# Expert stage: gate and value columns paired on a partition, one PSUM bank per expert, one-hots by comparison, one weight buffer fewer

## The chip, the cores and the metric

The kernel runs on one core of a Trainium2 chip. The metric is the device time of one execution in microseconds (us), median over runs. Before the change it is 1808.41 us (three runs, 1807.29 to 1809.11). In the profile PE is TensorE (matmuls and transposes), PEld its weight loads, DVE is VectorE, ACT is ScalarE, POOL is GpSimd, and SP is the engine whose queue issues the weight DMAs.

## The reference

The program computes two transformer blocks on 256 tokens of width 1024, with a context of 256 tokens, all in float32. The first block mixes retention and a long convolution and ends in a mixture of 32 experts, of which each token uses two. The second has two layers of its own. The change concerns the experts:

```
expert_id = g_star * EXPERTS_PER_GROUP + e_top
...
def expert_block(args):
    xblk, e = args
    return (jax.nn.silu(xblk @ w1[e]) * (xblk @ w3[e])) @ w2[e]
...
y = yb[dest] * sw[:, None].astype(u.dtype)
return jax.ops.segment_sum(y, stok, num_segments=n_tok)
```

`w1` and `w3` are 1024 by 512, `w2` is 512 by 1024, so one expert has 6 MB of weights and all 32 have 201 MB, each read once. The result is `x + gt2 * y`, then normed.

## The kernel before

**Order of the work.** `program` (L1745) runs the first block's mix, then `route_all` (L1021: positions and weights of every token for every expert) and `moe` (L1035: the experts), then the second block. While the experts run, `side()` puts one step of the generator `context_side` behind each expert: the context's layer of the second block. It is matmul work with split operands (`hh`, `hl`, `wh`, `wl`) that uses two PSUM banks of its own, "pf". The kernel is written in Tile, whose scheduler sets the order of each engine's instructions when the program is built; the hardware then runs each engine's list in that order.

**One expert** has up to 32 slots (tokens). `gather` (L945) makes, for a group of 4 or 8 experts (`GROUPS` 4, 4, 8, 8, 8), the one-hots `oh` of slots by comparing positions with a row of numbers, and with matmuls the slots' modulated rows `xg` [128 columns, 8, 32 n]. `expert` (L984) then does a first product of `xg` (stationary, 32 columns) with `w1` and `w3` (moving, 256 columns): 32 matmuls, four column blocks on four groups of 32 partitions. Since gate (`w1`) and value (`w3`) end on different partitions there, ACT copies the 128x256 result out (`eh`), PE transposes both halves into a second bank, ACT takes tanh (`eth`), DVE multiplies twice (`ex`), and the second product, 16 matmuls with `w2`, goes into a third bank. `put` (L1040) weights the result by slot weight and gate row (`ey`), splits it into `yh` and `yl`, and adds it to the four accumulators `acc` by matmuls with the scatter matrix `sc`.

`scatter_mat` (L969) makes `sc` for every expert: POOL copies the expert's one-hots four times over (`oh` 128x256), PE transposes them (two transposes), two matmuls with `wt` give the slots' weights `ws`, ACT copies both out.

**Banks.** `ps()` (L187) hands out PSUM tiles; in this stage it alternates two banks, "pm". An expert uses one for the first product, one for the transposes, one for the second product and one for `scatter_mat`, in turn.

**Weights.** `half` (L234) takes a buffer of 1 MB (128x2048), from a pool of 6 (`p16`) or one of `XB` = 4 more (`p16x`, made by `more_chunks`), and SP issues its load. An expert has six such halves; `w1`'s first, `w3`'s first, `w1`'s second, `w3`'s second, `w2`'s two. Each half of `w1` and `w3` holds four K tiles of 512 columns, and a buffer comes free after its last matmul. Halves of the context's layer take their turn in the same pools:

```
def half(self, src):
    self.nchunk += 1
    x = self.p16x and self.nchunk * self.nx % (6 + self.nx) < self.nx
    pool = self.p16x if x else self.p16
    t = pool.tile([P, 2048], F32, tag="T16", name=self.nm("w"))
    self.load(t, src)
    return t
```

SP's queue is in order: a load that waits for its buffer holds up all loads behind it. `phase` (L136) makes the other tile pools; `n2` is the number of 128x512 tiles of the stage (1 before).

## Time and profile before

| what | value |
|---|---|
| runs (us) | 1807.29, 1808.41, 1809.11 |
| profiled execution | 1809.11 us, its span 1809.1 us |
| PE / PEld busy | 1675.7 us (93%) / 1262.9 us (70%) |
| DVE / ACT / POOL busy | 982.5 us (54%) / 723.0 us (40%) / 97.1 us (5%) |
| granted clock of TensorE, mean | 0.975 |
| HBM | 487.43 MB read, 5.80 MB written, 273 GB/s |
| chain that ended last | PE 64%, DVE 4%, DMA 3%, issue 2%, ACT 2% |
| expert stage, first product of the first expert to end of the last | 466.6 to 1089.0 us |

The profiled execution is the slowest of the three runs, 0.7 us above the median; nothing lies outside its span. A line names the line of the kernel, the engine, the operation, output and inputs by their names in the program, and shapes. L200 is the helper that issues every matmul, L203 that of transposes, so tiles tell them apart: `pm<-w,xg` is a first product, `pm<-w,ex` a second, `pm<-ident,eh` the transposes of an expert's hidden columns, `pm<-ident,oh` and `pm<-wt,oh` the work of `scatter_mat`, `acc<-yh,sc` and `acc<-yl,sc` the sums, and `pf<-...` the context's layer. A float32 matmul stands as two or four records. "issue" as a releaser means that nothing the profile shows was waited for.

### The profile page before, as it was taken

To read this page: it belongs to the slowest core of one execution; us is meant where nothing else is said; L and a number is where in the kernel's file an instruction comes from. 1 tells how busy PE (TensorE), PEld (TensorE's weight loads), DVE (VectorE), ACT (ScalarE), POOL (GpSimd) and SP (SyncE) were. 2 spreads that over 40 slices of the span, in tenths; PEclk is the share of its full clock that TensorE was granted. 3 is DMA by queue.
4 is the path that set the end of the run, shared out by engine and by line. 5 is a ranking of instruction groups with operands and counts; after the bars stand their busy time and mean duration, and the time that the engine had idled before them with its cause. 6 is when DMAs were issued, how large, how long until landed. Compare 5 with 4: busy or idle time off the path is not lost.

```text
span 1809.1 us, 29140 instructions
## 1 busy us (share of the span) xinstructions
PE 1675.7 (93%) x11876; PEld 1262.9 (70%) x11876; DVE 982.5 (54%) x1747; ACT 723.0 (40%) x1246; POOL 97.1 (5%) x127
## 2 busy tenths in 40 slices
PE   5999999999888989999899989998999989979997
PEld 1678766668565556776676658775899768659996
DVE  5625556466224345454454457586655567755555
ACT  2413434343323333332232236463444445635443
POOL 0000000000000000000000002011000021110001
PEclk9899999998999999999999999999999999989998
DMA  9654678985799999899979997617555676235550
GB/s 372 265 210 163 229 268 314 345 314 211 298 420 420 405 396 369 335 422 420 399 304 422 406 378 226 213 66 285 210 192 190 232 229 204 98 111 190 191 189 35
DMA packets 79035, 495.18 MB, mean 274 GB/s; under 512 B 9024, under 2 KB 15840, under 8 KB 22832
## 3 DMA queue, kind: packets, MB, share of 16 engines
q1 hardware_dynamic: 73920, 475.94, 68.7%
q0 software_dynamic: 4000, 13.13, 2.8%
q10 hardware_dynamic: 976, 4.19, 0.6%
q8 instruction: 95, 1.56, 0.3%
q14 instruction: 44, 0.36, 0.1%
HBM read 487.43 MB, written 5.80 MB: 273 GB/s over the span
## 4 chain that ended last, share of the span: by engine, by line
PE 64%; DVE 4%; DMA 3%; issue 2%; ACT 2%; SPq 0%; ACTq 0%; DVEq 0%
PE pf L200 23%; PE pm L200 19%; PE acc L200 11%; PE pa L200 5%; PE pj L200 2%; PE pm L203 2%; DMA w<-in_w_in 1%; PE pf L203 1%; PE pada L200 1%; DMA w<-in_e 1%; DVE xn L213 0%; DVE x L1596 0%; DVE wl L273 0%; ACT eh L206 0%; DVE rq L218 0%
## 5 line engine op out<-in xcount | busy, mean ns | idle before, releaser
L206 ACT ACTIVATE wh<-w 128x1024 fp32r<-128x1024 f32 x350 | 367.2, 1057 | 399.8 <-PE pa L200 152.3
L273 DVE TENSOR_TENSOR wl<-w,wh 128x1024 fp32r<-128x1024 f32 x246 | 301.7, 1229 | 302.9 <-PE pa L200 100.3
L200 PE MATMUL pf<-hh,wh 128*128 128x256 f32 x592 | 168.4, 286 | 3.7 <-ACT wh L206 2.6
L200 PE MATMUL pf<-hl,wh 128*128 128x256 f32 x592 | 166.5, 283 | 0.0
L200 PE MATMUL pf<-hh,wl 128*128 128x256 f32 x592 | 165.1, 285 | 0.8 <-DVE wl L273 0.8
L209 DVE TENSOR_TENSOR wl<-w,wh 128x1024 fp32r<-128x1024 f32 x96 | 117.2, 1224 | 83.5 <-ACT a L206 29.5
L200 PE MATMUL pm<-w,xg 128*32 128x256 f32 x2048 | 133.0, 382 | 1.9 <-DMA w<-in_e 1.3
L200 PEld LDWEIGHTS pf<-hh,wh 128*128 128x128 f32 x592 | 113.2, 191 | 10.0 <-issue 4.1
L200 PEld LDWEIGHTS pf<-hh,wl 128*128 128x128 f32 x592 | 111.4, 191 | 3.7 <-DVE wl L273 1.2
L200 PEld LDWEIGHTS pf<-hl,wh 128*128 128x128 f32 x592 | 113.1, 191 | 1.0 <-issue 0.4
L200 PE MATMUL acc<-wl,hh 128*128 128x512 f32 x256 | 101.8, 398 | 0.0
L200 PE MATMUL acc<-wh,hl 128*128 128x512 f32 x256 | 101.3, 396 | 0.0
L200 PEld LDWEIGHTS pm<-w,xg 128*32 128x32 f32 x2048 | 64.8, 109 | 51.9 <-issue 11.9
L200 PE MATMUL pada<-w,csil 128*32 128x512 f32 x576 | 92.2, 621 | 5.0 <-DMA w<-in_ada_w 5.0
L200 PE MATMUL acc<-wh,hh 128*128 128x512 f32 x256 | 90.7, 396 | 0.0
L200 PE MATMUL pm<-w,ex 128*32 128x256 f32 x1024 | 65.2, 393 | 25.8 <-issue 24.1
L200 PE MATMUL pm<-hh,wh 128*128 128x256 f32 x256 | 72.4, 283 | 0.0
L200 PE MATMUL pm<-hl,wh 128*128 128x256 f32 x256 | 72.2, 282 | 0.0
L200 PE MATMUL pm<-hh,wl 128*128 128x256 f32 x256 | 72.0, 281 | 0.0
L200 PEld LDWEIGHTS pm<-w,ex 128*32 128x32 f32 x1024 | 34.9, 112 | 47.5 <-issue 31.4
L200 PE MATMUL pf<-wl,hh 128*128 128x512 f32 x160 | 65.3, 408 | 1.0 <-DVE wl L209 1.0
L200 PE MATMUL pf<-wh,hl 128*128 128x512 f32 x160 | 63.2, 395 | 0.0
(500 smaller groups left out, 3487.9 us busy)
## 6 DMA issues: line engine op xcount, KB each, us to landing
w<-in_e SPq DMA_DIRECT2D x192, 1024.0 KB, 10.6
w<-in_ff SPq DMA_DIRECT2D x96, 1024.0 KB, 5.0
w<-in_ada_w SPq DMA_DIRECT2D x72, 1024.0 KB, 6.9
w<-in_w_in SPq DMA_DIRECT2D x54, 1024.0 KB, 8.3
w<-in_w_out SPq DMA_DIRECT2D x16, 1024.0 KB, 7.4
w<-in_ret_w_o SPq DMA_DIRECT2D x4, 1024.0 KB, 4.9
w<-in_w_su SPq DMA_DIRECT2D x3, 1024.0 KB, 4.9
adab<-in_ada_b SPq DMA_DIRECT2D x9, 256.0 KB, 12.7
```

The source lines that it names most:

```text
L200: self.nc.tensor.matmul(out, lhsT, rhs, start=start, stop=stop, skip_group_check=True)
L203: self.nc.tensor.transpose(out, in_, self.ident)
L206: self.nc.scalar.activation(out, in_, f, **k)
L209: self.nc.vector.tensor_tensor(out, a, b, op=op)
L273: (self.nc.gpsimd if self.slow > 0 else self.nc.vector).tensor_tensor(lo[:, :w], src, hi[:, :w], op=ALU.subtract)
```

## The change

- **Weights.** `e1` and `e3` become one array `e13` [32, 128, 8192]. A K tile has 1024 columns, and blocks of 256 columns hold 128 gate and 128 value columns, so that gate and value of the same hidden column are on the same partition after the first product. A 1 MB half now holds two K tiles (8 matmuls), one half used after the other.
- **Expert.** ACT takes tanh of the gate columns from the first product (`eg`), DVE makes `eg` and `eh`, PE transposes once (128x128), into columns 256 to 384 of the same bank; DVE multiplies by `wr` (`ex`), the slots' weights on rows; the second product goes into columns 0 to 256 of the same bank. `ey` is a product with the gate row alone.
- **Scatter matrices.** `scatter_mats` makes them for two experts at once: two matmuls spread a row of `posT` (positions, transposed once in `route`) over all partitions, by a broadcast column of `pick`, and one DVE comparison with `slot` (the partition's number modulo 32) gives `sc` [128, 2, 256]. Copy, transposes and weight matmuls of `scatter_mat` go.
- **Slot weights.** `gather` multiplies the one-hots by `wt` (two DVE operations) and sums them over partitions with two matmuls with a column of 0.5 (the silu's factor), which ACT copies to `wr`.
- **Buffers.** `XB` goes from 4 to 3: nine weight buffers in the stage instead of ten. `n2` goes from 1 to 3. `overflow` (experts with over 32 tokens) reads `e13`.

The rest of the diff takes out comments and docstrings.

```
-XA, XB = 2, 4
+XA, XB = 2, 3
...
-        t = self.pr.tile([P, 512], F32, tag="AR", name="router")[:, :484]
+        t = self.pr.tile([P, 512], F32, tag="AR", name="router")[:, :485]
...
+        self.slot = t[:, 484:485]
...
+        p = self.ps()[:32, :256]
+        for t in range(2):
+            self.tr(p[:, t * P:(t + 1) * P], self.pos[:, t, :])
+        self.posT = self.keep([32, 256], F32R, "posT")
+        self.act(self.posT, p)
+        self.pick = self.keep([32, 32], F32R, "pick")
+        self.act(self.pick, self.ident[:32, :32])
...
-        return oh, xg
-
-    def scatter_mat(self, oh, e, i):
-        o4 = self.tx([P, 2, 4, 32], F32, "oh4")
-        self.nc.gpsimd.tensor_copy(o4, oh[:, :, i:i + 1, :].to_broadcast([P, 2, 4, 32]))
-        p = self.ps()
-        v = [o4[:, t].rearrange("p j c -> p (j c)") for t in range(2)]
         for t in range(2):
-            self.tr(p[:, t * P:(t + 1) * P], v[t])
+            self.tt(oh[:, t], oh[:, t], self.wt[:, t, es].unsqueeze(2).to_broadcast([P, n, 32]), ALU.mult)
+        p = self.ps()[:, :w]
+        half = self.sm([P, 1])
+        self.nc.vector.memset(half, 0.5)
         for t in range(2):
-            self.mm(p[:, 256:257], v[t], self.wt[:, t, e:e + 1], False, t == 1)
-        sc, ws = self.tx([P, 256], F32R, "sc"), self.sm([P, 1])
-        self.act(sc, p[:, :256])
-        self.act(ws, p[:, 256:257])
-        return sc, ws
-
-    def expert(self, xg, e, i, put):
+            self.mm(p, half.to_broadcast([P, P]), oh[:, t].rearrange("p e c -> p (e c)"), t == 0, t == 1)
+        wr = self.keep([P, 256], F32, "wr")
+        self.act(wr[:, :w], p)
+        return wr, xg
+    def scatter_mats(self, e):
+        p = self.ps().rearrange("p (i t) -> p i t", i=2)
+        for i in range(2):
+            self.mm(p[:, i], self.pick[:, e + i:e + i + 1].to_broadcast([32, P]), self.posT, i == 0, True)
+        sc = self.t2([P, 2, 256], F32R, "sc")
+        self.ts(sc, p, self.slot, None, ALU.is_equal)
+        return sc
+    def expert(self, xg, wr, e, i, put):
         a = self.a
-        w1, w3 = (Chunk([]) for _ in range(2))
-        for h in range(2):
-            for n, w in (("e1", w1), ("e3", w3)):
-                w.halves.append(self.half(a[n][e][:, 2048 * h:2048 * h + 2048]))
+        w13 = self.chunk(a["e13"][e], (P, 8192))
         w2 = self.chunk(a["e2"][e])
         p = self.ps()
         for k in range(8):
             for j in range(4):
-                w = (w1, w3)[j // 2]
-                o = k * 512 + (j % 2) * 256
-                self.mm(p[32 * j:32 * j + 32, :256], xg[:, k, 32 * i:32 * i + 32], w[:, o:o + 256], k == 0, k == 7)
-        h = self.tx([P, 256], F32, "eh")
-        self.act(h, p[:, :256])
-        p = self.ps()
-        for q in range(2):
-            self.tr(p[:, q * P:(q + 1) * P], h[:, q * P:(q + 1) * P])
-        pv = p[:, :256].rearrange("p (q w j c) -> p q w j c", q=2, w=2, j=2)
-        th = self.tx([P, 2, 2, 32], F32, "eth")
-        x1 = self.tx([P, 2, 2, 32], F32, "ex1")
-        self.act(th, pv[:, :, 0], AF.Tanh, scale=0.5)
-        self.stt(x1, th, 1.0, pv[:, :, 0], ALU.add, ALU.mult)
-        self.stt(x1, x1, 0.5, pv[:, :, 1], ALU.mult, ALU.mult)
-        p = self.ps()
+                o = k * 1024 + j * 256
+                self.mm(p[32 * j:32 * j + 32, :256], xg[:, k, 32 * i:32 * i + 32], w13[:, o:o + 256], k == 0, k == 7)
+        g, h = self.tx([P, P], F32, "eg"), self.tx([P, P], F32, "eh")
+        self.act(g, p[:, :P], AF.Tanh, scale=0.5)
+        self.stt(g, g, 1.0, p[:, :P], ALU.add, ALU.mult)
+        self.tt(h, g, p[:, P:256], ALU.mult)
+        q = p[:, 256:256 + P]
+        self.tr(q, h)
+        x1 = self.tx([P, 4, 32], F32, "ex")
+        self.tt(x1, q.rearrange("p (j c) -> p j c", j=4),
+                wr[:, 32 * i:32 * i + 32].unsqueeze(1).to_broadcast([P, 4, 32]), ALU.mult)
         for f in range(4):
             for j in range(4):
-                self.mm(p[32 * j:32 * j + 32, :256], x1[:, f % 2, f // 2, :],
+                self.mm(p[32 * j:32 * j + 32, :256], x1[:, f, :],
                         w2[:, f * 1024 + j * 256:f * 1024 + (j + 1) * 256], f == 0, f == 3)
         put(e, p)
...
-            self.stt(y, p[:, :256], ws, self.g4, ALU.mult, ALU.mult)
+            self.tt(y, p[:, :256], self.g4, ALU.mult)
...
-                        self.mm(acc[j][:, t], sc[r, t * P:(t + 1) * P], v[r], e == 0 and t == 0 and n == 0, e == 31)
+                        self.mm(acc[j][:, t], sc[r, e % 2, t * P:(t + 1) * P], v[r], e == 0 and t == 0 and n == 0, e == 31)
 
         e = 0
         for n in GROUPS:
-            oh, xg = self.gather(xn, A, B, e, n)
+            wr, xg = self.gather(xn, A, B, e, n)
             for i in range(n):
-                sc, ws = self.scatter_mat(oh, e, i)
-                self.expert(xg, e, i, put)
+                if i % 2 == 0:
+                    sc = self.scatter_mats(e)
+                self.expert(xg, wr, e, i, put)
...
-                        for n in ("e1", "e3"):
+                        for n in range(2):
                             w = tile_(1024, "w").rearrange("p (k c) -> p k c", k=8)
-                            self.load(w, a[n][ds].rearrange("o p (k h c) -> p (o k) h c", k=8, h=4)[:, :, f])
...
+                            self.load(w, a["e13"][ds].rearrange("o p (k m c) -> p (o k) m c", k=8, m=8)[:, :, 2 * f + n])
...
-            self.phase(es, 1, 0, 1, 5)
+            self.phase(es, 1, 0, 3, 5)
...
-                                    np.tile(rb, (P, 1))], 1)
-    d["e1"] = np.concatenate([_pack(w) for w in i["expert_w1"][0]])
-    d["e3"] = np.concatenate([_pack(w) for w in i["expert_w3"][0]])
+                                    np.tile(rb, (P, 1)), (np.arange(P, dtype=np.float32) % 32)[:, None]], 1)
+    both = np.stack([i["expert_w1"][0].reshape(32, 8, P, 4, P), i["expert_w3"][0].reshape(32, 8, P, 4, P)], 4)
+    d["e13"] = both.transpose(0, 2, 1, 3, 4, 5).reshape(32, P, 8192)
```

The build's order shows how the scheduler places this. PE, around the end of the first product of expert 27, before (`w_...` are halves, `ident_81` the identity for transposes):

```order
L200 MATMUL pm_9333<-w_9325,xg_8622 32x256 x2
L200 MATMUL pm_9333<-w_9327,xg_8622 32x256 x2
L203 MATMUL pm_9368<-ident_81,eh_9366 128x128 x2
L200 MATMUL pm_9376<-w_9329,ex_1759_9372 32x256 x8
L200 MATMUL pm_9376<-w_9331,ex_1759_9372 32x256 x8
...
L200 MATMUL pf_9420<-wh_9421,hl_9181 128x512
L203 MATMUL pm_9501<-ident_81,oh_1782_9499 128x128 x2
L200 MATMUL pm_9501<-wt,oh_1782_9499 128x1 x2
L200 MATMUL acc_3896<-yl_9396,sc_9317 128x256
```

Halves of `w1` and `w3` alternate, and three banks are in use. The same place in the changed program:

```order
L200 MATMUL pm_9066<-w_9056,xg_8389 32x256 x8
L200 MATMUL pm_9066<-w_9058,xg_8389 32x256 x8
L200 MATMUL pm_9066<-w_9060,xg_8389 32x256 x8
L200 MATMUL pm_9229<-posT,pick 128x256 x2
L203 MATMUL pm_9066<-ident_81,eh_9100 128x128
L200 MATMUL pm_9066<-w_9062,ex_9105 32x256 x8
L200 MATMUL pm_9066<-w_9064,ex_9105 32x256 x8
L200 MATMUL pf_9149<-wh_9151,hh_8924 128x512
```

The halves are used one after the other, one bank (`pm_9066`) serves the whole expert, and the two matmuls of the next pair's scatter matrices (`pm_9229`) stand between the first product and the transpose.

DVE in the same expert, before:

```order
L209 TENSOR_TENSOR hl_9181<-a_1744_9305,hh_9180 128x512
L218 SCALAR_TENSOR_TENSOR ex_1759_9372<-eth_9371,pm_9368 128x128
L218 SCALAR_TENSOR_TENSOR ex_1759_9372<-ex_1759_9372,pm_9368 128x128
L218 SCALAR_TENSOR_TENSOR ey_9393<-pm_9376,sm_9318,gate_520_2882 128x256
L209 TENSOR_TENSOR wl_9422<-w_9415,wh_9421 128x1024
L209 TENSOR_TENSOR yl_9396<-ey_9393,yh_9395 128x256
```

Nothing stands ahead of `ex` but the context's `hl`. And changed:

```order
L209 TENSOR_TENSOR hl_8925<-a_1621_9049,hh_8924 128x512
L213 TENSOR_SCALAR sc_9232<-pm_9229,router 128x512
L218 SCALAR_TENSOR_TENSOR eg_9099<-eg_9099,pm_9066 128x128
L209 TENSOR_TENSOR eh_9100<-eg_9099,pm_9066 128x128
L209 TENSOR_TENSOR ex_9105<-pm_9066,wr 128x128
L209 TENSOR_TENSOR ey_9123<-pm_9066,gate_520_2882 128x256
L209 TENSOR_TENSOR wl_9152<-w_9145,wh_9151 128x1024
L209 TENSOR_TENSOR yl_9126<-ey_9123,yh_9125 128x256
```

The comparison `sc` of the next pair stands ahead of this expert's `eg`. The same holds in experts 19, 21, 25 and 29; in the other odd experts it stands apart from this chain.

## Rows read from the trace of the kernel before

**Rows 1.** Page: busy time by engine; a DMA issue with KB and us to landing

```profile
PE 1675.7 (93%) x11876; PEld 1262.9 (70%) x11876; DVE 982.5 (54%) x1747; ACT 723.0 (40%) x1246; POOL 97.1 (5%) x127
...
w<-in_e SPq DMA_DIRECT2D x192, 1024.0 KB, 10.6
```

**Rows 2.** Busy time in stretches: PE, PEld, DVE, ACT, POOL, clock, DMA share, GB/s

```profile
500.00:525.00 25.00, 20.62 (x246) 14.83 (x246) 3.56 (x11) 5.28 (x15) 0.40 (x1) 1.00 1.01 420
...
750.00:775.00 25.00, 24.99 (x207) 20.23 (x210) 13.39 (x18) 6.58 (x11) 0.00 (x0) 1.00 0.76 307
...
950.00:975.00 25.00, 23.15 (x269) 16.22 (x268) 9.69 (x15) 8.41 (x16) 0.81 (x2) 1.00 1.01 422
```

**Rows 3.** Chain of waits, 466 to 1092: start us, us, what

```profile
504.78 19.76 DMA w<-in_w_in
...
660.71 15.95 DMA w<-in_e
```

**Rows 4.** Waits of PE, 466 to 1092: us in total, times, longest

```profile
PE pm L200 <- issue: 24.1, 19, 3.4
...
PE pm L203 <- ACT eh L206: 8.9, 19, 0.6
...
PE acc L200 <- ACT yh L206: 8.4, 14, 1.2
```

**Rows 5.** Timeline of PE in expert 27: start us, us, instruction, idle before

```profile
999.97 0.28 PE L200 MATMUL pf<-hl,wh 128*128 128x256 f32 x1
1000.09 0.28 PE L200 MATMUL pf<-hh,wl 128*128 128x256 f32 x1
...
1000.41 3.66 PE L200 MATMUL pm<-w,xg 128*32 128x256 f32 x64
1004.60 0.44 PE L203 MATMUL pm<-ident,eh 128*128 128x128 f32 x2 [0.53 <-ACT eh L206]
1006.10 1.93 PE L200 MATMUL pm<-w,ex 128*32 128x256 f32 x32 [1.06 <-issue]
...
1012.27 0.38 PE L203 MATMUL pm<-ident,oh 128*128 128x128 f32 x2
...
1012.92 0.39 PE L200 MATMUL acc<-yl,sc 32*128 32x256 f32 x4
```

**Rows 6.** Timeline of ACT in expert 27

```profile
1004.17 0.38 ACT L206 ACTIVATE eh<-pm 128x256 f32<-128x256 f32 x1 [1.77 <-PE pm L200]
1005.08 0.28 ACT L206 ACTIVATE eth<-pm 128x128 f32<-128x128 f32 x1 [0.53 <-PE pm L203]
```

**Rows 7.** Timeline of DVE in expert 27

```profile
1005.39 0.29 DVE L218 SCALAR_TENSOR_TENSOR ex<-eth,pm 128x128 f32<-128x128 f32 x1 [2.20 <-ACT eth L206]
1005.71 0.29 DVE L218 SCALAR_TENSOR_TENSOR ex<-ex,pm 128x128 f32<-128x128 f32 x1
1008.17 0.48 DVE L218 SCALAR_TENSOR_TENSOR ey<-pm,sm,gate 128x256 f32<-128x256 f32 x1 [2.17 <-PE pm L200]
```

**Rows 8.** Instructions by line and form, 466 to 1092: busy us, mean ns, idle before

```profile
L209 DVE TENSOR_TENSOR a<-pf,rowbc 128x512 f32<-128x512 f32 x36 | 24.8, 689 | 47.0 <-PE pf L200 47.0
...
L200 PE MATMUL pm<-oh,xn 128*128 128x256 f32 x96 | 23.2, 384 | 0.0
...
L215 DVE TENSOR_SCALAR xg<-pm,A,adac 128x256 f32<-128x256 f32 x12 | 6.5, 541 | 9.7 <-ACT xg L206 9.7
...
L215 DVE TENSOR_SCALAR xg<-pm,A,adac 128x128 f32<-128x128 f32 x4 | 1.6, 410 | 6.9 <-ACT xg L206 6.9
```

**Rows 9.** Timeline of SP's queue at two places; loads of the stage: first, last start

```profile
468.54 35.31 SPq L221 DMA_DIRECT2D w<-in_e  x20
...
949.87 1.55 SPq L221 DMA_DIRECT2D w<-in_e  x2
...
L221 SPq DMA_DIRECT2D w<-in_e x192: 327/328/1251, 388.4 to 1064.4; - x192
```

**Rows 10.** Timeline of PE where that load's first use stands

```profile
969.60 1.93 PE L200 MATMUL pm<-w,xg 128*32 128x256 f32 x32
```

More of the change, by code (lines that the diff above doesn't have):

```diff
@@ L832, in route_setup @@
     def route_setup(self, st):
-        t = self.pr.tile([P, 512], F32, tag="AR", name="router")[:, :484]
+        t = self.pr.tile([P, 512], F32, tag="AR", name="router")[:, :485]
         self.lsm(t, self.a["k_router"])
         self.iota, self.before = t[:, P:160], t[:, :P]
-        rw, rb = t[:, 160:448].rearrange("p (k n) -> p k n", k=8), t[:, 448:]
+        rw, rb = t[:, 160:448].rearrange("p (k n) -> p k n", k=8), t[:, 448:484]
+        self.slot = t[:, 484:485]
         self.A2, self.B2 = self.one([P, 8], F32, "A2", True), st[1][:, 0, 3, :]
@@ L1126, in overflow @@
                                 self.mm(ps, w[:, k], hT[:, k, :], k == 0, k == 7)
-                            if n == "e1":
+                            if n == 0:
                                 self.act(y[:, :P], ps, AF.Tanh, scale=0.5)
```

## The prediction

> **What bounds the kernel now.** I read the page first. [Rows 1] show TensorE (PE) busy for 93% of the span, so the questions are where PE stops and where the work that the change removes stands on PE's own path. The table of stretches comes next, because the change also takes a weight buffer away. [Rows 2] show three kinds of stretch in the expert stage: 500 to 525 us with the DMA at a share of 1.01 and 420 GB/s while PE is busy 20.6 of 25 us (weights are the limit), 750 to 775 with the DMA at 0.76 and PE at 25.0 (PE is the limit), and 950 to 975 with the DMA full again while PE has 23.2. The chain of waits says where weights end last: only two pieces of DMA stand in the chain of the whole stage, at 504.78 and 660.71 [rows 3]. So up to about 676 us (experts 0 to 12) the DMA sets the time, and from there to 1089 (experts 13 to 31) PE does, with the DMA catching up in its gaps.
>
> The waits of PE in the stage [rows 4] then say what its gaps are: 24.1 us in 19 gaps before an expert's second product, 8.9 us in 19 gaps before the transposes of its hidden columns, 8.4 us before the sums into `acc`. All three are the short chain inside an expert, which the change rewrites. Expert 27 shows it row by row [rows 5 to 7]. The first product ends at 1000.41 + 3.66 = 1004.07; ACT copies (0.38), PE transposes twice (0.44), ACT takes the tanh (0.28), DVE multiplies twice (0.29 each), and the second product starts at 1006.10: a chain of 2.03 us with nothing else on PE. Counted in PE's timeline, 14 of the experts 13 to 31 have this chain bare; in experts 13 to 17 rows of the context's layer stand in it and cover it.
>
> **The change part by part.**
> *Chain of an expert.* The copy of 256 columns and one transpose go; tanh now starts on the first product. In durations of [rows 5 to 7], with their hand-overs (0.11 PE to ACT, 0.03 on to DVE and between its operations, 0.05 to PE, 0.04 from PE, 0.10 from DVE to PE): 0.11 + 0.28 + 0.03 + 0.29 + 0.03 + 0.29 + 0.05 + 0.28 (one transpose; half of the pair is 0.22, so at most this) + 0.04 + 0.29 + 0.10 = 1.79. That is 0.24 less than 2.03.
>
> *Scatter matrices.* Two transposes and the weight column of one expert took PE from 1012.27 to 1012.92, 0.65 us [rows 5]. In their place each pair of experts has two single-pass matmuls of 256 columns; single-pass ones start 0.12 apart (999.97 to 1000.09, [rows 5]), so 0.24 a pair. The copy on POOL and the copies on ACT had slack and are worth nothing.
>
> *The new one-hot on DVE.* `sc` is one comparison of 128x512 from PSUM. It is not in the trace. Below: 0.69 (an operation of that size from PSUM); above: 0.80, since the tensor_scalar from PSUM went from 410 to 541 ns over 128 columns [rows 8], and 256 more columns add 0.26. I take 0.80, whose rows are of the same kind of operation. [...]
>
> What matters is where `sc` stands. In the changed order its matmuls follow the last first-product matmul of an odd expert on PE, and `sc` stands on DVE ahead of that expert's own `eg`: in experts 19, 21, 25, 27 and 29. `eg` cannot start before the next pair's scatter matrix is done. There the chain is 0.24 + 0.11 + 0.80 + 0.03 + 0.29 + 0.03 + 0.29 + 0.05 + 0.28 + 0.04 + 0.29 + 0.10 = 2.55, against 2.03 + 0.65 = 2.68 for what it replaces: 0.13 gained.
>
> *Late stretch, experts 13 to 31.* Five with `sc` in the chain: 5 x 0.13 = 0.65. Nine bare ones without it: 9 x (0.24 + 0.65) = 8.0. Five covered ones gain only the scatter work: 5 x 0.65 = 3.25. The matmuls of the four other pairs cost 4 x 0.24 = 1.0. The weights on rows add two full matmuls per group, each four records; a record of that width costs 23.2 / 96 = 0.24 [rows 8], so two groups cost 2 x 4 x 0.24 = 1.9, all on PE. Sum: 0.65 + 8.0 + 3.25 - 1.0 - 1.9 = 9.0 us less.
>
> *One weight buffer less.* A buffer holds 1.048 MB, 2.49 us at 421 GB/s [rows 2]. In the early stretch the DMA runs without a stop from the first release at 468.54 [rows 9], 1.9 us after the first product began. With nine buffers one chunk less is there at the start: 2.49 more to move. But in the new layout a half is done after 8 of the matmuls instead of 16 alternating ones, half of 1.9 us, so the DMA starts some 0.9 earlier. Bounds 0 and 1.6; I take 0.9, since the DMA is not quite unbroken there. PE's savings before 676 are waited away and count nothing. In the late stretch I cost the buffer at nothing: what hides it is the time between a chunk's landing and its use. One of the tightest there is issued at 949.87 and used at 969.60 [rows 9, 10]; with a median landing of 10.6 [rows 1] that leaves 9.1 us. A buffer comes free on average every (1064.4 - 468.5) / 182 = 3.3 us [rows 9] (the 192 loads less the ten buffers filled before), which is what the smaller ring takes off. If that cover were gone, the second rival follows.
>
> *Start of the stage.* Two more transposes and two copies for the slot rows, and the first group's extra multiplications, delay something between 0 and 1 us ahead of the first product; I take 0.5, as only the transposes are surely ahead on PE. Removed text and the later order of block 2 are costed at nothing.
>
> **Sum:** 1809.1 (the profiled execution, 0.7 above the median of 1808.4) - 9.0 + 0.9 + 0.5 = 1801.5 us.
>
> **The rivals.**
> *The gain is larger.* If DVE gets to `sc` without holding `eg` up (early matmuls, idle DVE), the five experts gain 0.89 each, 3.8 more, and the row weights lie in other gaps, 1.9 more: 1801.5 - 5.7 = 1795.8. For it: DVE has wide gaps [rows 2]. Against: the order on both engines is fixed, and PE is fed without gaps elsewhere.
>
> *Slower: nine buffers starve PE.* Place: the ends of the stretches in which the DMA is full, one early and three late. If there a chunk arrives one transfer late, each costs 2.49, and what PE saved before is waited away; only experts 28 to 31 keep about 2 us: 1809.1 + 1.6 + 3 x 2.49 - 2.0 = 1816. It decides where the time between landing and use falls under 3.3 us. Against: the 9.1 above. For: the DMA is at 1.01 for whole stretches, so that a loss is not made good soon, and PE that runs faster asks sooner. [...]
>
> *One PSUM bank per expert takes the gain back.* Before, an expert used three turns of the two banks, and its columns were copied out early; now its bank stays held until `ey` has read the second product. With two banks and one more use per pair, the first product of every even expert needs the bank of the odd one before it: a wait of 0.14 and `ey`'s 0.48 [rows 7], 0.62. Nine late pairs: 9 x 0.62 = 5.6, so 1801.5 + 5.6 = 1807.1. It decides where no rows of the context's layer stand between the second product and the next first one. Against: in expert 27 several us of such rows stand there. [...]
>
> *It doesn't do what it says.* The bytes moved are the same, and the order shows the removed rows gone; so the part that could fail is only the chain, which the third rival prices.
>
> **How the numbers follow.** My forecast has 0.56, the larger gain 0.14, starved weights 0.15, the held bank 0.15. The forecast's own spread is from 1797 to 1805 (sc at 0.69 or held longer, the early chunk at 0 or 1.6, the start at 0 or 1). The range leaves out the lowest part of the larger gain and most of the starved case: 1794 to 1813. A difference of 0.2%, 3.6 us, is about what a measurement of this kernel can tell from none. Faster by more than that (under 1804.8): nearly all of the forecast and of the larger gain, 0.68. Within it: most of the held bank and some of the forecast, 0.17. Slower: the starved case, 0.15.
>
> **What would show it.** Right: after 676 us the gap from the end of the first product to the second is near 1.8 us in even experts and near 2.5 in 19, 21, 25, 27, 29, with `sc` named as what DVE did; no idle of PE before a first product; no new DMA pieces in the chain after 680; the end of the stage about 7.6 us earlier, block 2 unchanged. Wrong: PE waiting for `w<-in_e` after 700 (too few buffers), first products waiting for `ey` (the bank), or a later stage that moves by microseconds.

## Result and profile after

The changed kernel takes **1829.49 us** (median of 4 runs, 1828.66 to 1830.19) against 1808.43 before: ratio 1.0113, 95% interval 1.0097 to 1.0128. It is 21 us slower where 7 us less were forecast, and outside the range given. The profiled execution took 1828.66 us, its span 1826.9.

Busy time and DMA issue on the page, in answer to [rows 1]:

```profile
PE 1677.4 (92%) x11706; PEld 1245.2 (68%) x11706; DVE 999.1 (55%) x1810; ACT 704.4 (39%) x1157; POOL 82.6 (5%) x95
...
w<-in_e SPq DMA_DIRECT2D x192, 1024.0 KB, 9.9
```

PE has 170 records less to do and is busy 1.7 us longer. That is a first sign: fewer records, on average a little slower. Where the time went, from the timelines of PE (start of the first product of expert 0, of the second products of experts 13 and 31, in us; the kernels e1 to e15 are told below):

| kernel | expert 0 | 13 | 31 | span |
|---|---|---|---|---|
| before | 466.6 | 707.2 | 1085.9 | 1809.1 |
| after | 473.7 | 720.0 | 1103.1 | 1826.9 |
| e2 (before, nine buffers) | 468.2 | 710.2 | 1091.8 | 1813.8 |
| e4 (before, paired columns) | 464.9 | 706.7 | 1081.9 | 1811.2 |
| e1 (branch) | 467.2 | 712.4 | 1096.8 | 1816.7 |
| e5 (branch, own bank) | 466.3 | 703.3 | 1085.9 | 1806.7 |
| e6 (as e4, own bank) | 464.6 | 707.1 | 1089.6 | 1807.9 |
| e10 (branch and sc) | 465.0 | 699.4 | 1078.5 | 1805.0 |
| e13 (small tiles, nine) | 465.7 | 699.4 | 1088.0 | 1812.2 |
| e14 (small tiles, ten) | 464.4 | 700.5 | 1085.6 | 1804.7 |
| e15 (no weights) | 465.0 | 699.7 | 1075.7 | 1803.3 |

The 17.8 us of the spans split into 7.1 ahead of the first product, 5.7 from there to expert 13, 4.4 from there to expert 31, and 0.6 behind it. The medians are 21 apart; of the 3 us that are missing here, 1.8 lie in that the profiled execution of the kernel before has nothing outside its span and all others have 1.8, so against "before" the spans of this table read some 1.8 us too short.

**Ahead of the first product.** DVE's timeline around the one-hots of the first group, of the kernel before:

```profile
451.20 0.23 DVE L209 TENSOR_TENSOR wt<-sm,sm 128x64 f32<-128x64 f32 x1
456.60 0.49 DVE L209 TENSOR_TENSOR oh<-router,pos 128x128 f32<-128x128 f32 x2 [5.17 <-PEq L1106]
```

and of the changed kernel:

```profile
453.96 0.23 DVE L209 TENSOR_TENSOR wt<-sm,sm 128x64 f32<-128x64 f32 x1
457.56 0.42 DVE L1285 TENSOR_REDUCE sm<-pf 128x1 f32<-128x256 f32 x1 [3.38 <-PE pf L200]
463.18 0.49 DVE L209 TENSOR_TENSOR oh<-router,pos 128x128 f32<-128x128 f32 x2 [5.20 <-PEq L1112]
```

Between `wt` and `oh` lies the branch of `overflow`, through which every engine goes. In both kernels DVE gets its next work 5.2 us after its last work ahead of the branch (451.43 to 456.60, 457.98 to 463.18). That is not a constant of the branch: in e1 and e11 below it is 3.5 and 9.2. What DVE waits for is named in the brackets, PE's queue at the branch. PE's own branch instruction is a long one (all instructions of the branch's line; duration in ns, start in us), before

```profile
L1106 PEldq COMPARE_BRANCH  x1: 3725/3725/3725, 452.7 to 452.7; - x1
```

and after:

```profile
L1112 PEldq COMPARE_BRANCH  x1: 4765/4765/4765, 458.2 to 458.2; - x1
```

On the other engines it takes 0.05 to 0.07 us. In the kernel before it starts while rows of the context's layer still run on PE, up to 455.88, and they cover most of it. In the changed kernel the transposes of the positions (456.59) and a row of the context's scores stand ahead of it on PE, and the copy of the positions on ACT. PE reaches the branch 0.7 us after its last row had ended, and the 4.8 us lie bare. PE's timeline, of the kernel before and of the changed one:

```profile
457.03 1.35 PE L200 MATMUL pm<-oh,xn 128*128 128x128 f32 x10 [1.14 <-DVE oh L209]
```

```profile
463.61 0.98 PE L200 MATMUL pm<-oh,xn 128*128 128x128 f32 x3 [6.09 <-DVE oh L209]
466.54 5.12 PE L200 MATMUL pm<-oh,xn 128*128 128x128 f32 x29 [1.95 <-issue]
```

That is 6.09 us of idle against 1.14. Behind it the clock is down. Stretches of the kernel before (PE, PEld, DVE, ACT, POOL, granted clock, DMA share, GB/s):

```profile
460.00:470.00 10.00, 8.71 (x102) 6.35 (x100) 3.25 (x10) 4.78 (x15) 0.00 (x0) 1.00 0.48 179
470.00:700.00 230.00, 206.36 (x2076) 134.57 (x2069) 86.32 (x218) 78.61 (x198) 9.39 (x19) 0.99 1.00 412
700.00:1080.00 380.00, 352.09 (x3386) 261.37 (x3388) 189.47 (x301) 120.33 (x214) 8.57 (x19) 1.00 0.94 381
```

and of the changed one:

```profile
460.00:470.00 10.00, 4.44 (x19) 4.18 (x20) 0.92 (x4) 0.56 (x2) 0.00 (x0) 0.50 0.05 15
470.00:700.00 230.00, 199.53 (x2033) 121.28 (x2033) 91.49 (x246) 68.36 (x163) 4.22 (x6) 0.96 0.98 404
700.00:1080.00 380.00, 352.82 (x3192) 250.96 (x3190) 194.63 (x304) 110.33 (x159) 0.00 (x0) 0.98 0.92 368
```

Three readings. From 460 to 470 the DMA stands (0.05): no buffer comes free before the first product. From 470 to 700, where weights are the limit, 404 GB/s flow instead of 412: over 230 us 1.8 MB less, nearly two chunks. From 700 to 1080 PE is as busy as before with 194 records less, at a granted clock of 0.98 instead of 1.00 (the window is the same in time; the work in it begins some 13 us earlier in the changed kernel).

**The chain itself came out as forecast.** PE's timeline in expert 27, and in expert 28:

```profile
1021.61 0.50 PE L200 MATMUL pm<-posT,pick 32*128 32x256 f32 x2
1023.46 0.33 PE L203 MATMUL pm<-ident,eh 128*128 128x128 f32 x1 [1.36 <-DVE eh L209]
1024.17 1.93 PE L200 MATMUL pm<-w,ex 128*32 128x256 f32 x32 [0.38 <-DVE ex L209]
...
1044.83 0.33 PE L203 MATMUL pm<-ident,eh 128*128 128x128 f32 x1 [1.04 <-DVE eh L209]
1045.54 1.93 PE L200 MATMUL pm<-w,ex 128*32 128x256 f32 x32 [0.38 <-DVE ex L209]
```

and DVE's in expert 27:

```profile
1022.14 0.75 DVE L213 TENSOR_SCALAR sc<-pm,router 128x512 fp32r<-128x512 f32 x1 [1.30 <-PE pm L200]
1022.81 0.27 DVE L218 SCALAR_TENSOR_TENSOR eg<-eg,pm 128x128 f32<-128x128 f32 x1
1023.12 0.29 DVE L209 TENSOR_TENSOR eh<-eg,pm 128x128 f32<-128x128 f32 x1
```

The first product of expert 27 ends at 1021.68, the second begins at 1024.17: 2.49, with `sc` (0.75) ahead of `eg` as the order had it. In expert 28 it is 1.04 + 0.33 + 0.38 = 1.75. PE's waits in the whole stage, against [rows 4]:

```profile
PE pm L203 <- DVE eh L209: 24.8, 21, 1.9
PE acc L200 <- ACT yh L206: 9.2, 13, 2.1
PE pm L200 <- DVE ex L209: 7.4, 19, 0.5
...
PE pm L200 <- DMA w<-in_e: 4.2, 3, 2.4
```

The three stops of an expert add up to 41.4 us, just what they were (24.1 + 8.9 + 8.4). The two ahead of a second product are shorter in an even expert (1.04 + 0.38, against 0.53 + 1.06 in [rows 5]) and longer in an odd one (1.36 + 0.38); and which chains are covered has changed: in the kernel before 7.4 us of the context's rows stand in experts 18 and 24, in the changed one these two are bare and from 18 on only experts 23 and 31 have some rows in theirs. The DMA is named for 4.2 us, all of it up to 684.

### The profile page after: what moved, and what is told of

Read it like the earlier page. It is cut to its first block, busy times and chain, and to the rows that moved or that the text cites. A ratio compares the mean times of both kernels' runs of the same rounds, so it can differ in the third digit from the quotient of the medians.

```text
span 1826.9 us, 28657 instructions
## 1 busy us (share of the span) xinstructions
PE 1677.4 (92%) x11706; PEld 1245.2 (68%) x11706; DVE 999.1 (55%) x1810; ACT 704.4 (39%) x1157; POOL 82.6 (5%) x95
## 4 chain that ended last, share of the span: by engine, by line
PE 62%; DVE 6%; DMA 3%; ACT 2%; issue 1%; SPq 0%; DVEq 0%; ACTq 0%
PE pf L200 22%; PE pm L200 18%; PE acc L200 11%; PE pa L200 5%; PE pj L200 2%; DMA w<-in_e 2%; PE pf L203 1%; PE pada L200 1%; PE pm L203 1%; DVE wl L273 1%; DVE rq L218 1%; DVE x L1602 0%; DMA k_d<-planes 0%; DVE a L209 0%; ACT e L206 0%
## 5 line engine op out<-in xcount | busy, mean ns | idle before, releaser
L200 PE MATMUL pf<-hh,wh 128*128 128x256 f32 x592 | 167.9, 285 | 0.4 <-ACT wh L206 0.4
L200 PE MATMUL pf<-hh,wl 128*128 128x256 f32 x592 | 165.3, 285 | 1.4 <-DVE wl L273 1.4
L200 PE MATMUL pf<-hl,wh 128*128 128x256 f32 x592 | 166.5, 283 | 0.0
L200 PE MATMUL pm<-w,xg 128*32 128x256 f32 x2048 | 139.5, 385 | 5.7 <-DMA w<-in_e 4.2
L200 PEld LDWEIGHTS pf<-hh,wh 128*128 128x128 f32 x592 | 112.9, 191 | 5.0 <-issue 2.1
L200 PEld LDWEIGHTS pf<-hh,wl 128*128 128x128 f32 x592 | 111.2, 190 | 6.9 <-issue 3.3
L200 PEld LDWEIGHTS pf<-hl,wh 128*128 128x128 f32 x592 | 112.7, 190 | 1.3 <-issue 0.4
L200 PEld LDWEIGHTS pm<-w,xg 128*32 128x32 f32 x2048 | 64.3, 110 | 63.7 <-issue 18.7
L200 PE MATMUL acc<-wl,hh 128*128 128x512 f32 x256 | 101.8, 398 | 0.0
L200 PE MATMUL acc<-wh,hl 128*128 128x512 f32 x256 | 101.3, 396 | 0.0
L200 PE MATMUL pada<-w,csil 128*32 128x512 f32 x576 | 91.1, 614 | 4.3 <-DMA w<-in_ada_w 4.2
L200 PE MATMUL acc<-wh,hh 128*128 128x512 f32 x256 | 90.7, 396 | 0.0
L200 PE MATMUL pm<-w,ex 128*32 128x256 f32 x1024 | 69.7, 411 | 7.4 <-DVE ex L209 7.4
L200 PE MATMUL pm<-hh,wh 128*128 128x256 f32 x256 | 72.8, 284 | 1.0 <-ACT hh L206 1.0
L200 PE MATMUL pm<-hl,wh 128*128 128x256 f32 x256 | 72.7, 284 | 0.0
L200 PE MATMUL pm<-hh,wl 128*128 128x256 f32 x256 | 72.2, 282 | 0.0
L200 PE MATMUL pf<-wl,hh 128*128 128x512 f32 x160 | 64.7, 404 | 0.9 <-DVE wl L209 0.9
L200 PE MATMUL pf<-wh,hh 128*128 128x512 f32 x160 | 63.7, 416 | 1.0 <-ACT pad L206 1.0
L200 PE MATMUL pf<-wh,hl 128*128 128x512 f32 x160 | 62.8, 397 | 0.0
```

The lines of the kernel that those rows point to most:

```text
L200: self.nc.tensor.matmul(out, lhsT, rhs, start=start, stop=stop, skip_group_check=True)
```

## The experiments

**One part undone or done alone.** Four theories were open at first: the work ahead of the branch, the missing buffer, the held PSUM bank, and `sc` in the chain. The kernel before was run beside each set of experiments, with medians from 1806.20 to 1809.79 us, and the ratios are to those runs; a difference between medians of different sets is sure to some 3 us only.

e1_branch makes `posT` and `pick` behind the branch instead of ahead of it:

```diff
-        p = self.ps()[:32, :256]
-        for t in range(2):
-            self.tr(p[:, t * P:(t + 1) * P], self.pos[:, t, :])
...
             self.overflow(x, xn)
+        p = self.ps()[:32, :256]
+        for t in range(2):
+            self.tr(p[:, t * P:(t + 1) * P], self.pos[:, t, :])
...
```

> The changed kernel with one edit: the transposed positions and the picking columns are made behind the branch of overflow instead of ahead of it, so no row of the context's scores stands on DVE ahead of the branch any more. Theory A (the late branch costs some 7 us of the 21): the first product starts near 467 instead of 473.7 us, and the time falls by 6 to 7 us, to 1822 to 1824. Rival (the weights set the early stretch anyway, so a later first product is free): the first product starts earlier, but the time stays within 2 us of 1829.5.

Measured: 1817.95 us, ratio 1.0059 (1.0046 to 1.0072), 11.5 less than the change. DVE's timeline:

```profile
454.85 0.23 DVE L209 TENSOR_TENSOR wt<-sm,sm 128x64 f32<-128x64 f32 x1
458.59 0.49 DVE L209 TENSOR_TENSOR oh<-router,pos 128x128 f32<-128x128 f32 x2 [3.52 <-PEq L1112]
```

The one-hots come 4.6 us earlier, the first product 6.5 us (467.2). The clock stays at 1.00 from 460 to 470. On PE rows run to 457.64 and 1.07 us of idle follow at the branch, which is covered again. Of the 28 us between forecast and result, 11.5 by the medians (9.8 by the ratios) are the place of two transposes and two copies, more than the 6 to 7 of theory A: the profiles put 6.5 at the start and 3.9 behind expert 31, where nothing was edited.

e2_before_nine takes one buffer from the kernel before, e3_after_eight one more from the changed one:

```diff
-XA, XB = 2, 4
+XA, XB = 2, 3
```

> The kernel before with nine weight buffers instead of ten and nothing else. Theory B (a buffer is dear, it is the main cost of the change): 1816 to 1820, with PE waiting for weights after 700 us. Rival (a buffer is worth one transfer in the early stretch, 2.5 us, and nothing later): 1808 to 1811.

> The changed kernel with eight weight buffers instead of nine. Theory B (buffers are dear): the time rises by 8 to 12 us, to 1838 to 1842. Rival (one transfer in the early stretch): 1830 to 1833.

Measured: 1815.55 (1.0048, 1.0034 to 1.0061), 7.5 us for the tenth buffer; and 1829.36 (1.0115, 1.0096 to 1.0134), nothing for the ninth, within the some 4 us that these intervals leave open. In e2 the table shows 1.6 us lost ahead of the first product, 1.3 from there to expert 13 and 2.9 between experts 13 and 31. The first of these is not a load that came late: the built order is another ahead of the branch, and the one-hots `oh` come at 459.16 instead of 456.60. The total is just short of theory B, but the wait that it named is not there: from 690 on PE waits nowhere for `w<-in_e` in e2. The loads that come late are those of the context's layer. ACT's waits for them from 690 to 1110, of the kernel before and of e2:

```profile
ACT wh L206 <- DMA w<-in_ff: 2.7, 1, 2.7
```

```profile
ACT wh L206 <- DMA w<-in_ff: 12.3, 2, 6.9
```

The buffer is priced here with the order that comes with it, and not yet inside the change.

e4_pair_ten is the kernel before with paired columns and the short chain only: old scatter matrices, weights on `ey`, ten buffers; e6_pair_banks gives its second product a bank of its own; e5_branch_banks does that to e1.

```diff
-        h = self.tx([P, 256], F32, "eh")
-        self.act(h, p[:, :256])
...
+        self.act(g, p[:, :P], AF.Tanh, scale=0.5)
+        self.stt(g, g, 1.0, p[:, :P], ALU.add, ALU.mult)
+        self.tt(h, g, p[:, P:256], ALU.mult)
...
+        self.ts(x1, q.rearrange("p (j c) -> p j c", j=4), 0.5)
```

```diff
+        p = self.ps()
         for f in range(4):
             for j in range(4):
                 self.mm(p[32 * j:32 * j + 32, :256], x1[:, f, :],
```

> The kernel before with only the paired columns and the short chain in one PSUM bank: scatter matrices and slot weights as before (the factor 0.5 is applied where the weights on rows were), ten buffers. Theory C (the short chain does gain): 14 bare experts by 0.24 us, so 1805, between 1803 and 1807. Rival D (one bank per expert, or the order that the scheduler makes of it, takes the gain back): 1808 to 1816.

> The fourth experiment's kernel (kernel before, paired columns, ten buffers, old scatter matrices) with the second product in a bank of its own. Theory C (the chain gains 0.24 us in 14 experts and one bank costs nothing): as the fourth experiment in the stage, late stretch 375 us. Rival D (the held bank cost something there): late stretch 370 to 373. The end of the stage to the end of the program, 729 us there against 723 before, tells whether block 2 follows the turn of the banks: if it does, 723 comes back and the total is 1804 to 1807.

> The first experiment's kernel (positions transposed behind the branch) with the second product in a bank of its own again. In the built order the matmuls of the next pair's scatter matrices then stand behind the second product's first rows instead of between the first product and the transpose, and sc stands behind ex instead of ahead of eg. Theory C2 (sc in the chain of the odd experts makes PE's stops long, and after such stops the granted clock falls in the rows that follow): no fall of the clock between 830 and 1030, the late stretch (second product of expert 13 to that of 31) 384 us becomes 375 to 379, total 1809 to 1813. Rival (the late loss is the ninth buffer's, as PE asks sooner): the late stretch stays above 382, total 1816 to 1819.

Measured: e4 1816.65 (1.0053, 1.0039 to 1.0067), e6 1808.97 (1.0004, 0.9991 to 1.0017), e5 1811.35 (1.0024, 1.0011 to 1.0037). In e4's profile the late stretch takes 375.2 us instead of 378.7. The 3.5 are what 14 bare chains of 0.24 would give, but that is partly luck: PE's timeline shows nine bare chains there, 1.75 us each at best, and e6 with the same short chain takes 382.5. And the stage is followed by a stretch that takes 6.1 us longer (729.3 instead of 723.2), so nothing is left. A bank of its own takes 6.6 us off e1 and 7.7 off e4. That is the size of the rival's 5.6, but not its place: late, where the rival put it, e5 gains 1.8 of e1's 384.4 and e6 loses 7.3. e5's total lies in the range of theory C2, but the late stretch that was to give it (375 to 379) did not; e6 came out in neither of its two ranges, e4 just above its rival's.

**The clock.** The granted clock had fallen from 0.975 to 0.965 over the span. If PE's many short stops cause that and with it the loss, rows without use that fill the stops should give time back. e7_branch_fill puts four transposes behind the first products of experts 18 to 31 of e1, e8_banks_fill five behind the first and five behind the second products of e5, e9_pair_fill five behind the first products of e6.

```diff
+        if e > 17:
+            for _ in range(4):
+                self.tr(p[:, 384:512], self.ident)
```

> The first experiment's kernel with four throwaway transposes of the identity into unused columns of the expert's bank, behind the first product of experts 18 to 31: PE has rows where it stopped before. They delay sc in five odd experts by some 0.6 us. Theory C2 (the clock falls after the stops): the falls between 830 and 1030 go or get fewer, and the stage is not longer although rows were added: 1814 to 1818. Rival (the clock has nothing to do with these stops): the falls stay and the time rises by 2 to 4 us, to 1820 to 1822.

> The fifth experiment's kernel (branch free, second product in its own bank, nine buffers) with five throwaway transposes behind the first product and five behind the second, in experts 18 to 31, where PE stopped 1.04 and 0.99 us. Theory C2 (the granted clock falls after the stops and that is what is lost): the falls near 870 and 1030 go, and the time comes down by 1 to 4 us although 140 rows were added: 1807 to 1811. Rival (rows added cost what they last, the falls come anyway): 1812 to 1816.

> The sixth experiment's kernel (before, paired columns, ten buffers, three banks, old scatter matrices) with five throwaway transposes behind the first product of experts 18 to 31. Theory C2: the fall near 985 goes and the chain's gain shows: 1804 to 1807, faster than before. Rival: 1808 to 1812.

Measured: e7 1816.68 (1.0051, 1.0034 to 1.0068), 1.3 less than e1; e8 1827.48 (1.0092, 1.0075 to 1.0109), 16 more than e5; e9 1815.75 (1.0036, 1.0023 to 1.0050), 7 more than e6. From 700 to 1080 the clock of e7 is 0.99 where e1 has 0.98, that of e8 1.00 where e5 has 0.99. So the rows do go with a higher clock, but in e8 and e9 they cost more than that gives (outside both expected ranges), and e7's 1.3 us less, inside theory C2's range, are hardly clear of the noise. They don't stay in the gap. In e7 (PE's timeline)

```profile
1012.81 0.66 PE L203 MATMUL pm<-ident 128*128 128x128 f32 x4
1013.40 0.50 PE L200 MATMUL pm<-posT,pick 32*128 32x256 f32 x2
1015.26 0.33 PE L203 MATMUL pm<-ident,eh 128*128 128x128 f32 x1 [1.36 <-DVE eh L209]
```

the transposes write the bank that tanh reads, tanh waits for them (ACT's row names PE's transposes, for 2.19 us), the chain begins 0.6 us later, and PE's stop of 1.36 us is as long as it was. These runs neither clear nor convict the clock.

**The sc matrices.** e10_branch_sc is e1 with the two matmuls of a pair's scatter matrix in a bank of the other rotation (`pf`); e11_sc_only does that to the change, without e1's edit; e12_both_banks adds e5's bank to e10.

```diff
-        p = self.ps().rearrange("p (i t) -> p i t", i=2)
+        p = self.pf.tile([P, 512], F32, tag="F", name=self.nm("pf")).rearrange("p (i t) -> p i t", i=2)
```

> The first experiment's kernel, one bank per expert as in the change, but the scatter matrices' matmuls go to the banks of the context's layer. In the built order they then stand amid the first product or behind the transpose, and sc is made before eg could start: it leaves the chain while the expert's bank stays held. Theory C3 (sc in the chain is what cost): as the fifth experiment, 1810 to 1813. Rival D2 (the held bank is what cost, and the fifth experiment gained by the separate bank): as the first, 1816 to 1819.

> The changed kernel with one edit only: the scatter matrices' matmuls go to the banks of the context's layer (as in the tenth experiment), positions are transposed ahead of the branch as in the change. In the built order sc stands ahead of eg in four experts instead of eight, in these four behind matmuls that come amid the first product, and the context's score matmul, which stood ahead of the branch, now stands behind it; the two transposes of positions stay ahead. If the score's row on DVE was what held the branch up: first product near 467, total 1807 to 1811. If the transposes and copies of positions were: first product near 473, total 1816 to 1820.

> The tenth experiment's kernel with the second product in a bank of its own as well: a try for a version that beats both kernels. If a held bank still costs something: 1802 to 1806. If it costs nothing once sc is out of the chain: 1806 to 1810, as the tenth.

Measured: e10 **1807.72** (0.9998, 0.9984 to 1.0013), 10.2 less than e1; e11 1823.44 (1.0089, 1.0068 to 1.0111), 6.1 less than the change; e12 1820.45 (1.0077, 1.0049 to 1.0105, its runs from 1810.91 to 1827.86). e10 beat both of its ranges, e12 missed both upward; e11's start came as the second theory had it, its total 3 us above. Stretches of e1, early, and of e10:

```profile
470.00:700.00 230.00, 202.17 (x1974) 123.64 (x1967) 91.30 (x239) 67.44 (x157) 4.22 (x6) 0.96 0.99 402
```

```profile
470.00:700.00 230.00, 204.95 (x2036) 125.27 (x2031) 95.72 (x247) 69.49 (x162) 4.21 (x6) 0.99 1.01 418
700.00:1080.00 380.00, 355.73 (x3320) 250.92 (x3312) 200.68 (x337) 111.96 (x166) 1.64 (x3) 0.98 0.94 379
```

The weights flow at 418 GB/s, more than before (412). PE's waits for `eh` from 700 to 1110, of the change and of e10:

```profile
PE pm L203 <- DVE eh L209: 15.8, 13, 1.9
```

```profile
PE pm L203 <- DVE eh L209: 8.0, 8, 1.4
```

Two things change in e10 at once, and these runs don't part them: the matmuls no longer take a turn of the two `pm` banks, and `sc` mostly stands away from `eg` on DVE. e5 says something of it. There the pair's matmuls keep their turn of `pm`, but `sc` stands behind `ex` in every late expert, and no late chain holds it. Against e1 that build gains 8.2 us from the first product to expert 13 and only 1.8 in the late stretch, where e10 gains 10.8 and 5.3. So most of the gain is early, and `sc` in the chain is not shown to be all of the late part. In e11 the first product still starts at 472.7, though there the context's row stands behind the branch. So it is the positions' transposes and copies that hold the branch up. PE passes it under cover again there (its rows run to 457.52, and 0.85 us of idle follow at the branch), but ACT reaches it only behind its copy. The branch on ACT, ACT's and DVE's timelines of e11:

```profile
L1112 ACTq COMPARE_BRANCH  x1: 45/45/45, 460.1 to 460.1; - x1
```

```profile
457.88 0.36 ACT L206 ACTIVATE posT<-pm 32x256 fp32r<-32x256 f32 x1
```

```profile
463.94 0.49 DVE L209 TENSOR_TENSOR oh<-router,pos 128x128 f32<-128x128 f32 x2 [9.21 <-SPq L1112]
```

DVE was ready at 454.73 and got its work 5.7 us after the copy of the positions had ended on ACT.

e12 speaks against the held bank: with `sc` out of the rotation a bank of its own makes e10 12.7 us slower, though e12's runs are far apart. In e5 and e6 a bank of its own gave 6.6 and 7.7 us. The order that the scheduler makes differs in each of these builds, so a bank's own price stays open.

**The buffer and the weights, inside the change.** The change gave the tenth buffer's place to its small tiles. e13_small_nine lays those out in less memory (one tile for gate, value, scaled columns and result; weights in the tile of the one-hots; positions in 16 bits), e14_small_ten is the same with ten buffers, e15_no_weights is e10 without the weights on rows.

```diff
-        g, h = self.tx([P, P], F32, "eg"), self.tx([P, P], F32, "eh")
+        big = self.p2.tile([P, 256], F32, tag="eg", name=self.nm("eg"))
+        g = big[:, :P]
...
-        wr = self.keep([P, 256], F32, "wr")
+        wr = full[:, 0].rearrange("p e c -> p (e c)")
...
-            self.phase(es, 1, 0, 3, 5)
+            self.phase(es, 1, 0, 1, 2)
```

```diff
-XA, XB = 2, 3
+XA, XB = 2, 4
```

```diff
-        for t in range(2):
-            self.mm(p, half.to_broadcast([P, P]), oh[:, t].rearrange("p e c -> p (e c)"), t == 0, t == 1)
...
-        self.tt(x1, q.rearrange("p (j c) -> p j c", j=4),
-                wr[:, 32 * i:32 * i + 32].unsqueeze(1).to_broadcast([P, 4, 32]), ALU.mult)
+        self.ts(x1, q.rearrange("p (j c) -> p j c", j=4), 0.5)
```

> The version of e10_branch_sc (positions behind the branch, scatter matmuls in a bank of the other rotation) with its small tiles laid out in less memory: the weights of the slots stand in the tile of the one-hots, gate, value and scaled columns and the weighted result share one tile per expert, positions in 16 bits. Nine weight buffers, as in the change. Theory of the three prices (branch, sc in the chain, one buffer): as e10_branch_sc, 1807.7, within 4 us. Rival (the order of the loads and small tiles matters more than the three parts): off by more than 6 us from it, to either side.

> The same with ten weight buffers, as the kernel before has. If the missing buffer costs here what it cost the kernel before (7.5 us in e2_before_nine, of which its profile showed 1.6 at the start and 2.9 in the late stretch), 1800 to 1804. Rival (nine buffers cost the changed kernel nothing, as eight cost nothing more in e3_after_eight): within 2 us of e13_small_nine.

> The version of e10_branch_sc without the weights on transposed rows: it leaves out the weights of the slots, every slot counts as weight 1. Price of the prediction for the rows (1.9 us late, nothing early): 1805 to 1806. Rival (the rows, which stand between the groups' products and behind a wait for DVE, cost more, 2 to 3 us a group): 1800 to 1803. If the time is within 1 us of e10_branch_sc the rows are covered.

Measured: e13 1811.52 (1.0025, 1.0009 to 1.0041), e14 **1806.59** (0.9999, 0.9987 to 1.0011), e15 1804.15 (0.9976, 0.9964 to 0.9988). e13 is within the 4 us of its theory; e14 and e15 fell between their two ranges. The tenth buffer is worth 4.9 us at an otherwise equal layout. The two profiles are 7.5 apart (table): 1.3 at the start, 3.5 between experts 13 and 31, 5.1 behind 31, against 2.4 more from the first product to expert 13. PE's waits for weights, of e13 and of e14:

```profile
PE pm L200 <- DMA w<-in_e: 3.8, 4, 1.4
```

```profile
PE pm L200 <- DMA w<-in_e: 1.8, 3, 0.9
```

So only 2 us of it show as a wait of PE for weights, all ahead of 690. Behind that it is again ACT that waits for the context's weights, 14.9 us in e13 and nothing in e14:

```profile
ACT wh L206 <- DMA w<-in_ff: 14.9, 3, 8.3
```

How much of the late price comes by this way is not shown: e10 has 11.5 us of the same wait and is as fast as e14. The weights on rows cost 3.6 us by e15 against e10 (3.1 between experts 13 and 31). No version here beats the kernel before and computes the same: e10 and e14 equal it.

## Why the prediction was wrong

**Chain of an expert: right.** 1.79 was worked out, 1.75 measured; 2.55 with `sc` ahead, 2.49 and 2.50 measured in 27 and the other odd ones (3.04 in 21, where the granted clock is 0.66 from 885 to 890); `sc` 0.749 on average between the bounds 0.69 and 0.80. What the shorter chain is worth over the late stretch stays open: 3.5 us less in e4, 3.8 more in e6. The count of covered chains was right by number only: 14, 15, 16, 18 and 24 are the covered ones in the kernel before, not 13 to 17, and in the changed order they are others.

**Scatter matrices: right in kind, mis-sized.** The pair's two matmuls were priced at 0.24 of PE; 32 of them are recorded with 328 ns each, and from the end of the first product to the end of the pair 0.43 us pass. That is under a microsecond for the four pairs.

**Start of the stage: this step failed first.** "Two more transposes and two copies ... delay something between 0 and 1 us ahead of the first product; I take 0.5." It was 7.1 in the profile, and undoing it gave 6.5 there and 11.5 in the median. The duration of the work was right; what it stands ahead of got no term. PE's branch instruction takes 3.7 us in the kernel before and rows already under way cover most of it. In the changed kernel the added work holds PE back until those rows are done and 4.8 us lie bare; in e11 it holds ACT back. The one-hots come at 463.18 and 463.94 instead of 456.60 and everything behind them later, the first release of a buffer included, and from there on this kernel loads weights without a stop (DMA share 1.00 from 470 to 700 before). The timeline of the kernel before shows the place: DVE idle for 5.17 us behind PE's queue at the branch.

**Where sc stands: the second step that failed.** The prediction gave the pair's matrix a place in five late chains and counted five gains of 0.13 there; against the chain without `sc` that is 0.76 lost each, 3.8 us, and a rival counted that back. On DVE `sc` stands right ahead of `eg` in eight experts, 4, 5 and 9 besides those five, and the early ones were counted at nothing. Moving its matmuls to the other rotation gave 10.2: by the profiles of e1 and e10 5.3 us late, 10.8 between the first product and expert 13, 2.2 at the start, with 6.6 given back behind expert 31. "PE's savings before 676 are waited away and count nothing" does not hold for PE's losses: there the DMA needs a buffer every 2.49 us, and with PE late the loads fell from 418 to 402 GB/s (e10 and e1, from 470 to 700). The granted clock is lower there too, 0.96 against 0.99; which of the two comes first these runs don't show, nor how much is `sc` on DVE and how much the turn of the banks.

**One buffer less: mis-sized.** 0.9 with bounds of 0 and 1.6 at the start, late nothing. Measured 7.5 in the kernel before and 4.9 in the changed one; by their profiles 2.9 and 3.5 in the late stretch, which had been costed at nothing. The 1.6 and 1.3 at the start look like the bound, but that is luck: they stand ahead of the first product, where the one-hots come 2.6 and 2.4 later, and not in the loads behind it, where the term was meant (from the first product to expert 13, 1.3 more in e2, 2.4 less in e13 than in e14). The rival of the nine buffers was right that the late stretch pays, and wrong in how: from 690 on PE waits nowhere for `w<-in_e`, neither in the changed kernel nor in e2 or e13; ACT waits for the context's `w<-in_ff` in e2 and e13, which the ring also carries. The way from the buffer to the late price stays open. The 9.1 us between a landing and its use, one of the tightest found, did not bound the cost. A ninth buffer taken away cost nothing more that could be measured (e3), so the price seems not to be one per buffer either.

**Weights on rows: mis-sized.** 1.9 forecast, 3.6 measured, 3.1 in the late stretch.

**The sum.** From 1829.5, taking the branch (11.5) and `sc` (10.2) off gives 1807.7, and the tenth buffer at 4.9 would leave 1802.8, near the 1801.5 forecast. That is a sum of prices from different builds. It was not measured as one kernel: e14 has all three edits, but in the small-tile layout, which costs 3.8 us itself by e13 against e10, and stands at 1806.6. In the late stretch 383.1 - 5.3 (`sc`) - 3.5 (buffer) - 1.2 (rows above their price) is 373.1, where 378.7 - 9.0 = 369.7 was forecast; 3.4 us stay without a name (4.7, if one starts from e10's own 379.1). The clock is a candidate: to three digits it is 0.982 instead of 0.996 over the 380 us, which is 5 us of full clock less; but e10 shows 0.98 there too.

**The rivals.** The larger gain (1795.8) was the wrong sign. The starved nine buffers (1816) had the right sign, but the buffer is 5 to 7 us of 21. The held bank (1807.1) is not borne out: e5 and e6 gain by a bank of their own, but not where the rival had it, e12 loses by it, and e10, as fast as the kernel before, holds the bank. "The end of the stage about 7.6 us earlier" was 17.2 later; "block 2 unchanged" holds for the change (0.6 us) but not for its parts, where 719.9 us follow the start of expert 31's second product in e1 and 726.5 in e10, whose stage ends earlier; why is not shown.

## What to carry to other kernels

Before an edit adds small work, look for a point that all engines pass together (here a branch) and at which side of it the work lands: two transposes and two copies of under a microsecond moved the stage by 7 us there and the total by some 11, and moving seven lines gave them back. In the stretch that the DMA limits here, PE's delays were not free: the queue of the loads waits there for PE's matmuls (`SPq L221 <- PE pm L200`, 119.9 us in 42 waits from 470 to 700 in the kernel before), and with PE late the loads fell from 418 to 402 GB/s (e10 and e1). A ring whose main reader shows hardly a wait on its loads can still be short: in e2 the tenth buffer was worth 7.5 us, and from 690 on PE waited nowhere for `w<-in_e`. So look at who else loads through it, take a buffer from the kernel *before* and time it ahead of trading one for anything.

## What the runs showed of the hardware

The branch of `overflow` takes PE longer than the other engines: 3.7 us in the kernel before and 4.8 in the changed one, against 0.05 to 0.07 on the rest. Rows that were already under way on PE ran on meanwhile (to 455.88 in the kernel before, whose branch lasts from 452.7 to 456.4).

Stops of about one microsecond, close together, were followed by a lower clock in some places and not in others. In e10, PE's timeline in expert 27 and behind it:

```profile
999.84 0.33 PE L203 MATMUL pm<-ident,eh 128*128 128x128 f32 x1 [1.02 <-DVE eh L209]
...
1003.48 0.39 PE L200 MATMUL acc<-yh,sc 32*128 32x256 f32 x4 [0.99 <-ACT yh L206]
...
1005.69 0.80 PE L200 MATMUL pf<-wl,hh 128*128 128x512 f32 x1 [0.46 <-DVE wl L209]
1006.28 0.63 PE L200 MATMUL pf<-wh,hl 128*128 128x512 f32 x1
1006.71 0.63 PE L200 MATMUL pf<-wl,hh 128*128 128x512 f32 x1
...
1009.10 0.40 PE L200 MATMUL pf<-wl,hh 128*128 128x512 f32 x1
1009.34 0.40 PE L200 MATMUL pf<-wh,hl 128*128 128x512 f32 x1
```

and the stretches there (columns as above):

```profile
1000.00:1005.00 5.00, 3.55 (x51) 1.85 (x50) 1.73 (x4) 1.99 (x3) 0.00 (x0) 1.00 1.01 428
1005.00:1010.00 5.00, 4.54 (x13) 3.26 (x12) 2.18 (x3) 1.50 (x3) 0.00 (x0) 0.66 1.01 424
```

From 1006.28 to 1008.84 the same matmuls start 0.43 apart instead of 0.24: the clock is lower for some 3 us, and its mean over the 5 us from 1005 is 0.66. This came after 5 us in which PE was busy for 3.55. But the same chain in expert 21, with stops of 1.04 and 0.99 us, left the clock as it was:

```profile
865.00:870.00 5.00, 2.58 (x41) 1.27 (x37) 1.57 (x5) 1.01 (x3) 0.00 (x0) 1.00 0.96 359
870.00:875.00 5.00, 5.00 (x46) 3.39 (x42) 2.97 (x4) 2.83 (x4) 0.00 (x0) 1.00 1.01 423
```

So the stops alone do not decide it.

The same program also runs at different clocks from run to run, and its time goes with it: e11 took 1816.43 us at a mean clock of 0.971 and 1829.71 at 0.964. Before has span times clock 1809.1 x 0.975 = 1763.9, after 1826.9 x 0.965 = 1763.0. Counted in clocks that TensorE was granted, the two kernels are equally long (0.001 of clock is 1.8 us), although after has less to do. Whether the clock is cause or companion of the stops, the filled kernels did not settle.
